# A two-layer hybrid model on one core: the second layer's modulation vector moves from TensorE to VectorE, with other first loads, slot sizes and orders

## The chip, the cores and the metric

The kernel runs on one core of a Trainium2 chip. The time is device microseconds (us) of one execution. Three runs of the kernel before are known, and one execution taken with the profiler. Engines are named as in the profile: PE is TensorE, DVE is VectorE, ACT is ScalarE, POOL is GpSimd, SP is the engine that issues the DMAs.

## What is computed

Two layers over 384 tokens (128 of a prompt, 256 latent ones), model width 1024, all in fp32. From the reference, cut:

```python
mod_ctx = silu(c_ctx) @ w_ada[l] + b_ada[l]     # for the 128 prompt tokens
mod_lat = silu(c) @ w_ada[l] + b_ada[l]         # for the 256 latent tokens
shift1, scale1, gate1, shift2, scale2, gate2 = split(mod, 6)
h = rms_norm(x) * (1 + scale1) + shift1
out = mix(h)     # w_in; SSD scan, attention and mLSTM side by side; gated merge; w_out
x = x + gate1 * out
h = rms_norm(x) * (1 + scale2) + shift2
a_, b_ = split(h @ w_ffn_in, 2)                 # 2 x 2816 columns
x = x + gate2 * ((silu(a_) * b_) @ w_ffn_out)
# after both layers: final rms_norm; also new k, v and the scans' end states
```

The piece that matters most here is the first pair of lines ("adaLN"): per layer two vectors of 1024 (prompt and latent) times a matrix of 1024 x 6144. It depends on c and c_ctx alone, not on x.

## The kernel before, in words

All large weights come in one stream `ws` of pieces of 128 x 1024 floats (512 KB), in the order in which `stream()` (line 64) lists them. A piece is loaded into one of four buffers `raw`. To keep fp32 precision, it is split into a high part (`wh`, a rounding copy on ACT) and a low part (`wl` = raw - wh, a subtraction on DVE, or on POOL for the pieces that `POOL_SPLIT` names, one of so many of a kind). The activations are split in the same way: `HH` and `HL`, in the FFN the slots `A` and `C`. A dense product of one piece is 24 matmuls: eight blocks of 128 rows, each high by high, high by low and low by high, over 384 columns (386 with the slots A and C, which carry two more) into one of `ND` = 3 PSUM tiles `d`.

The stages of a layer are: input projections and the three branches interleaved with gates, the branches' projections (`br`), the output projection (`out`), then the FFN: `ff` with 44 pieces, `fa` and `fb` in turn, and `fo` with 22. In ff, each tile d is evacuated on DVE (`sc<-d,nacc`), a product of the two halves is made (`sc<-sc,sc`), the shift of the modulation is added (a pair of `sc<-sc,sh,sc`, 128 and 256 columns), and the hidden block is split into high and low part (`F<-sc,F` and the like for other slots).

adaLN. Layer 0's first pieces are wanted at once: `ada` (line 733) runs 16 pieces through PE at the start, 4 x 4, with the conditioning `silc` (32 columns, two used) as one operand, and transposes what comes out. The rest is done in steps, `ada_step` (line 754): 2 pieces, 8 matmuls `m<-raw,silc`; after 8 steps ScalarE copies the rows out, and four transposes with an addition of the bias `bada` bring the result into columns `mod`. There are 40 steps. 16 are layer 0's and lie in the branches' projections, 24 are layer 1's and lie in layer 0's FFN, 16 in ff and 8 in fo.

What sets the order. All operations are first recorded (`Recorder.rec`, which is why nearly every row of the profile names line 509, where they are emitted) and then ordered by `order()` (line 376): a list scheduler with a table of costs, in which a ready operation with the lowest key goes first. The key is the place in the program plus an urgency: `FEED` (weights), `EVAC` (evacuations), `DENSE`. The result is a fixed list per engine, and each engine runs its own list in order; an instruction that waits holds up all behind it. All DMAs go through SP's list. SBUF slots have letters (`A` to `F2`, `K`, `HH`, `HL`, `PH`, `PL`) and are used for different things in turn; at the start only `PH` (the input x) is in use of the large ones.

At the seam from `out` to the FFN, `outproj` (line 1358) adds the gated result to x and sums squares; `norm_end` (835) forms the reciprocal root (a chain of small DVE operations on 128 x 3, `rs`), spreads it over partitions with a matmul (`m<-sc,ones`), and ACT stores it as `nacc`. FFN matmuls start before that, on unnormalised data; the evacuation multiplies by `nacc`.

Of the kernel before, what the change touches and what calls it, by code (L numbers as in the profile page):

```python
# [31 lines left out]
EARLY_GATES = (0, 1, 2, 4, 5, 5, 6, 6, 6, 10, 11, 13, 13, 23, 32, 32, 32, 33, 33, 37, 37, 37, 37, 38)  # L32
# [31 lines left out]
def stream():  # L64
# [3 lines left out]
    for l in range(LAYERS):  # L68
# [18 lines left out]
        s += spread(ff, steps(l + 1, 0, 1)) + spread(fo, steps(l + 1, 2)) if l + 1 < LAYERS else ff + fo  # L87
# [135 lines left out]
class Recorder:  # L223
# [152 lines left out]
    def order(self):  # L376
# [25 lines left out]
        port = ring = 0.0  # L402
# [133 lines left out]
MIX = "sssiiiqqqsqqmamsasqamsasammmaamam"  # L536

POOL_SPLIT = {"inn": 4, "fa": 3, "fo": 3}


class Net:
    def __init__(self, ctx, tc, I, O):
# [237 lines left out]

    def setup(self):
# [8 lines left out]
        self.badas = []  # L790
        for l in range(LAYERS):
            b = self.const(f"bada{l}", [P, 48])
            self.dma(b, I["cols"][l, :, COLS["bada"][0]:COLS["bada"][0] + 48])
            self.badas.append(b)
# [813 lines left out]
```

## Time and profile before

| | us |
|---|---|
| median of 3 runs | 1937.8 (1936.15 to 1947.53) |
| the profiled execution | 1940.55, its span 1938.4, mean granted clock 0.994 |
| PE busy in the span | 1894.3 (98%) |
| DVE busy | 1290.6 (67%) |
| ACT busy | 945.6 (49%) |
| POOL busy | 367.1 (19%) |

PE's 98% is the first thing to read: nearly all of the time is matmul time, with short holes. Matmuls are pipelined, so a row's length (0.34 us) is longer than the distance to the next start (0.17 us); distances between starts give the pace. The same holds for DVE, where a row ends a little after the next one starts. A timeline row shows start, length, engine, line, operation, and in brackets how long the engine was idle before it and what ended that.

### The profile page before, as it was taken

The numbers are of one execution on the slowest core, as the hardware profiler recorded it, in microseconds if no ns is written. First come the engines' busy times: TensorE is split into PE (matmuls) and PEld (weight loads), VectorE is DVE, ScalarE is ACT, GpSimd is POOL, SyncE is SP. The second block draws the span as 40 slices with busy tenths as digits, with TensorE's granted clock in tenths as the row PEclk, the third lists the DMA queues.
The fourth block names the chain that finished last, engine by engine and source line by source line (L and its number), as shares of the span: only waits on it lengthen the run. The fifth ranks groups of instructions, "written<-read, shape, count | busy, mean of one in ns | idle before, by whom it ended". The sixth has DMA issues, their size and how long they took to land. (4 is left out here: it accounts for less than half of the span.)

```text
span 1938.4 us, 30576 instructions
## 1 busy us (share of the span) xinstructions
PE 1894.3 (98%) x11202; PEld 1728.1 (89%) x11202; DVE 1290.6 (67%) x2733; ACT 945.6 (49%) x1910; POOL 367.1 (19%) x355
## 2 busy tenths in 40 slices
PE   6999999999999999999999999999999999999997
PEld 4998898688888999999999978986889999999997
DVE  3856887986745666565348668978867567666622
ACT  3655565765422444444336546656655434444421
POOL 0115432210102210000211234322100022000121
PEclk9999999999999999999999999999999999999998
DMA  8466555554578666666654655555544555444441
GB/s 302 122 178 190 148 150 147 141 147 129 172 262 267 223 196 185 196 201 201 192 178 144 156 170 150 158 147 135 144 124 140 161 169 160 120 125 124 131 125 61
DMA packets 120342, 318.33 MB, mean 164 GB/s; under 512 B 13824, under 2 KB 57216, under 8 KB 119424
## 3 DMA queue, kind: packets, MB, share of 16 engines
q1 hardware_dynamic: 120192, 316.38, 54.8%
q8 instruction: 88, 1.44, 0.3%
q14 instruction: 62, 0.51, 0.1%
HBM read 295.54 MB, written 19.74 MB: 163 GB/s over the span
## 5 line engine op out<-in xcount | busy, mean ns | idle before, releaser
L509 ACT ACTIVATE wh<-raw 128x1024 fp32r<-128x1024 f32 x374 | 396.0, 1059 | 566.8 <-PE d L509 509.1
L509 DVE TENSOR_TENSOR wl<-raw,wh 128x1024 fp32r<-128x1024 f32 x335 | 437.3, 1306 | 247.3 <-ACT wh L509 240.4
L509 PE MATMUL d<-HH,wh 128*128 128x384 f32 x1448 | 493.0, 348 | 2.6 <-ACT sc L509 1.6
L509 PE MATMUL d<-HL,wh 128*128 128x384 f32 x1416 | 467.9, 336 | 1.4 <-DVE HL L509 1.4
L509 PE MATMUL d<-HH,wl 128*128 128x384 f32 x1384 | 465.6, 336 | 0.7 <-DVE wl L509 0.7
L509 PEld LDWEIGHTS d<-HH,wh 128*128 128x128 f32 x1448 | 272.6, 189 | 22.8 <-issue 14.8
L509 PEld LDWEIGHTS d<-HL,wh 128*128 128x128 f32 x1416 | 266.8, 189 | 3.2 <-DVE HL L509 1.7
L509 PEld LDWEIGHTS d<-HH,wl 128*128 128x128 f32 x1384 | 261.0, 189 | 1.1 <-DVE wl L509 1.1
L509 PE MATMUL d<-A,wh 128*128 128x386 f32 x744 | 254.8, 342 | 0.0
L509 PE MATMUL d<-C,wh 128*128 128x386 f32 x744 | 251.5, 338 | 0.0
L509 PE MATMUL d<-A,wl 128*128 128x386 f32 x744 | 250.1, 336 | 0.0
L509 POOL TENSOR_TENSOR wl<-raw,wh 128x1024 fp32r<-128x1024 f32 x39 | 93.9, 2409 | 449.6 <-ACT sh L509 361.3
L509 PEld LDWEIGHTS d<-A,wh 128*128 128x128 f32 x744 | 139.9, 188 | 13.0 <-issue 10.9
L509 PEld LDWEIGHTS d<-C,wh 128*128 128x128 f32 x744 | 140.6, 189 | 0.4
L509 PEld LDWEIGHTS d<-A,wl 128*128 128x128 f32 x744 | 139.9, 188 | 0.0
L509 POOL TENSOR_TENSOR sc<-sc,sc 128x126 f32<-128x126 f32 x112 | 66.7, 614 | 253.9 <-DVE sc L509 195.9
L509 DVE TENSOR_TENSOR sc<-d,nacc 128x384 f32<-128x384 f32 x93 | 51.8, 557 | 78.9 <-PE d L509 74.6
L509 DVE SCALAR_TENSOR_TENSOR PH<-PL,n,cst 128x128 f32<-128x128 f32 x288 | 95.9, 366 | 7.7 <-PE m L509 5.2
L509 PE MATMUL d<-wh,HH 128*128 128x512 f32 x240 | 98.2, 409 | 0.0
L509 PE MATMUL d<-wl,HH 128*128 128x512 f32 x240 | 93.9, 391 | 0.0
L509 PE MATMUL d<-wh,HL 128*128 128x512 f32 x240 | 93.8, 391 | 0.0
L509 DVE SCALAR_TENSOR_TENSOR sc<-d,cw,sc 128x127 f32<-128x127 f32 x224 | 79.2, 408 | 14.9 <-ACT sc L509 14.4
(237 smaller groups left out, 3080.1 us busy)
## 6 DMA issues: line engine op xcount, KB each, us to landing
raw<-in_ws SPq DMA_DIRECT2D x470, 512.0 KB, 3.9
PL<-rowr SPq DMA_DIRECT2D x48, 384.0 KB, 5.7
gd<-sc SPq DMA_DIRECT2D x48, 192.0 KB, 2.0
pb<-gd SPq DMA_DIRECT2D x48, 192.0 KB, 2.9
ex<-rowe SPq DMA_DIRECT2D x32, 128.0 KB, 4.1
ex<-rowe SPq DMA_DIRECT2D x16, 256.0 KB, 5.5
PH<-in_xT SPq DMA_DIRECT2D x2, 1536.0 KB, 7.2
yad<-pb SPq DMA_DIRECT2D x16, 192.0 KB, 3.0
```

Of the source, the lines that this page charges most:

```text
L509: tc.keep_in_program_order(getattr(engines[op.eng], meth)(*[real(a) for a in args], **{k: real(v) for k, v in kw.items()}))
```

## The change

1. *Layer 1's adaLN* is no longer done in steps on PE. Its 48 pieces come as 48 blocks (`ada_block`): each gives 128 columns of the result for both vectors by two scalar_tensor_tensor on DVE, raw times a row that is the same in all partitions (silu of c or c_ctx, read back from DRAM into the slot `PL`), with the sum over the row written to `mod`. 32 blocks lie in ff and 16 in fo. The weights are laid out anew for it.
2. *First loads.* The 16 first pieces no longer go through `raw` but come in six DMAs of two or three pieces into the slots A, C, E, F, D, PL, the first eight pieces with urgency `FIRST` and the last eight with `SECOND`; three pieces of the dense work load between them. The two bias loads come later; the setup has urgency `FIRST`.
3. *Norms* (`ssq` at the start, `norm_end`) get the urgency `NORM`, ahead of FEED.
4. *FFN low parts* of the hidden blocks of layer 0 (22 of 128 x 384) go from DVE to POOL, and `POOL_SPLIT` keeps only fo, now every second piece.
5. *Slots*: A, C and E get 3136 floats per partition, a multiple of 256 bytes, and the large slots a pool of their own with a pad of 64 bytes ahead.
6. *Order*: another interleaving of the branches (`MIX`), one gate one place earlier, and other costs in the scheduler.

```diff
-EARLY_GATES = (0, 1, 2, 4, 5, 5, 6, 6, 6, 10, 11, 13, 13, 23, 32, 32, 32, 33, 33, 37, 37, 37, 37, 38)
+EARLY_GATES = (0, 1, 2, 4, 5, 5, 6, 6, 6, 10, 11, 13, 13, 23, 31, 32, 32, 32, 33, 33, 37, 37, 37, 38)
...
-        s += spread(ff, steps(l + 1, 0, 1)) + spread(fo, steps(l + 1, 2)) if l + 1 < LAYERS else ff + fo
+        if l + 1 < LAYERS:
+            blocks = [(("adv", l + 1, place, j), 1) for place in range(6) for j in range(8)]
+            at = len(blocks) * len(ff) // len(ff + fo)
+            s += spread(ff, blocks[:at]) + spread(fo, blocks[at:])
+        else:
+            s += ff + fo
...
+            if "accum_out" in kw:
+                n += 60
...
-            return 0.36, rows * (0.025 + run * 4 * 0.0000415) / 16, 1.3 + min(rows, 256) * 0.0085
+            return 0.36, rows * (0.036 + run * 4 * 0.0000337) / 16, 1.3 + min(rows, 256) * 0.0085
...
+NORM = -90000
+
+FIRST, SECOND = -120000, -110000
...
+BIG = ("A", "B", "C", "D", "E", "F", "F2", "K", "HH", "HL", "PH", "PL")
+PADS = dict(p1=0, p2=64)
...
+AHEAD_OF_SECOND = 3
+
+FIRST_LOADS = ((0, 3, "A"), (3, 3, "C"), (6, 2, "E"), (8, 3, "F"), (11, 3, "D"), (14, 2, "PL"))
...
-MIX = "sssiiiqqqsqqmamsasqamsasammmaamam"
-
-POOL_SPLIT = {"inn": 4, "fa": 3, "fo": 3}
+MIX = "ssiiiqqqaqqmamsasqmssasasmmmaamam"
+
+POOL_SPLIT = {"fo": 2}
...
     def ada(self, l, u):
-        raws = self.piece(("ada", l, u), split=False)
+        key, cnt = self.stream[self.spos]
+        assert key == ("ada", l, u), key
+        self.spos += 1
+
+        if self.ppos % 8 == 0:
+            with self.urgency(SECOND if self.ppos else FIRST):
+                for pos, n, tag in FIRST_LOADS:
+                    if pos // 8 == self.ppos // 8:
+                        home = self.slot(tag, [P, n, 1024])
+                        self.dma(home.rearrange("p n c -> p (n c)"),
+                                 self.I["ws"][pos:pos + n].rearrange("n p c -> (n p c)").rearrange("(p m) -> p m", p=P))
+                        self.homes += [home[:, i] for i in range(n)]
+        raws = [self.homes.pop(0) for _ in range(cnt)]
...
+    def ada_block(self, kind, l, place, j):
+
+        if self.spos == self.adv_at:
+            t = self.slot("PL", [P, 3, D])
+            self.dma(t[:, 0:2], self.sild.rearrange("r p k -> r (p k)").unsqueeze(0).to_broadcast([P, 2, D]))
+            self.silb = t
+        raw, = self.piece((kind, l, place, j), split=False)
+        with self.urgency(FEED):
+            for r in range(2):
+                self.nc.vector.scalar_tensor_tensor(self.silb[:, 2] if r == 0 else raw, raw, 1.0, self.silb[:, r],
+                                                    ALU.mult, ALU.mult, accum_out=self.mod_col(l, place, j, r))
...
-            self.xs = [self.slot(t, [P, KT, NTOK + 2], F32R) for t in "AC"]
+            self.xs = [self.slot(t, [P, 3136], F32R)[:, 0:3088].rearrange("p (k n) -> p k n", k=KT) for t in "AC"]
...
-                self.tt(homes[j][:, 1], th, homes[j][:, 0].bitcast(F32), ALU.subtract)
+                (self.ptt if l == 0 else self.tt)(homes[j][:, 1], th, homes[j][:, 0].bitcast(F32), ALU.subtract)
...
-            self.norm_end(EPS)
+            with self.urgency(NORM):
+                self.norm_end(EPS)
```

How the lists move is seen at three places. In the rows the first number behind a name is the buffer, the second the version.

*The start, on PE.* Before, the last matmuls of `ada` read two `raw` buffers that are loaded one after the other, and dense matmuls (HH by wh) follow a transposition:

```order
L509 MATMUL d_37_315<-raw_33_266,silc_7_82 32x128 x8
L509 MATMUL d_37_315<-raw_34_276,silc_7_82 32x128 x8
L509 MATMUL m_58_346<-sc_57_334,ones_6_78 128x384
L509 MATMUL d_37_315<-raw_35_287,silc_7_82 32x128 x8
L509 MATMUL d_37_315<-raw_36_302,silc_7_82 32x128 x8
L509 MATMUL d_39_386<-cst_3_95,sc_38_382 128x128
L509 MATMUL d_73_407<-HH_60_368,wh_71_389 128x384
L509 MATMUL d_73_407<-HL_61_380,wh_71_389 128x384
L509 MATMUL d_73_407<-HH_60_368,wl_72_399 128x384
L509 MATMUL d_73_407<-HH_60_368,wh_71_389 128x384
```

In the change (line 516 now) the last sixteen read what one DMA brings into the slot PL, and three dense matmuls stand ahead of the transposition:

```order
L516 MATMUL d_27_308<-F_24_115,silc_8_93 32x128 x24
L516 MATMUL d_27_308<-D_25_117,silc_8_93 32x128 x8
L516 MATMUL d_30_361<-D_25_117,silc_8_93 32x128 x4
L516 MATMUL d_29_366<-cst_3_95,sc_28_359 128x128
L516 MATMUL d_30_361<-D_25_117,silc_8_93 32x128 x12
L516 MATMUL d_30_361<-PL_26_119,silc_8_93 32x128 x16
L516 MATMUL d_66_399<-HH_53_299,wh_64_254 128x384
L516 MATMUL d_66_399<-HL_54_304,wh_64_254 128x384
L516 MATMUL d_66_399<-HH_53_299,wl_65_269 128x384
L516 MATMUL d_32_403<-cst_3_95,sc_31_397 128x128
```

What moved: the operands are slots that are filled by six loads, and the dense product begins behind the last of them as before.

*The entry of layer 0's FFN, on DVE.* Here `rs` and `r` are the end of the reciprocal root, `sc<-cst,r` makes the matrix that PE spreads, `sc<-d,nacc` is an evacuation. Before:

```order
L509 SCALAR_TENSOR_TENSOR r3_1322_7359<-rs_1325_7338,rs_1326_7332 128x3
L509 TENSOR_SCALAR sc_1327_7361<-cst_3_95,r3_1322_7359 128x128 x2
L509 TENSOR_TENSOR wl_1362_7369<-raw_1360_7237,wh_1361_7351 128x1024
L509 TENSOR_SCALAR sc_1327_7361<-cst_3_95,r3_1322_7359 128x128
L509 TENSOR_TENSOR sc_1344_7395<-d_1342_7291,nacc_1321_7390 128x384
L509 TENSOR_TENSOR sc_1350_7411<-d_1348_7347,nacc_1321_7390 128x384
L509 SCALAR_TENSOR_TENSOR sc_1351_7418<-sc_1351_7418,sc_1344_7395 128x384
L509 SCALAR_TENSOR_TENSOR sc_1351_7418<-sc_1350_7411,sh_1349_7416,sc_1351_7418 128x128
```

In the change:

```order
L516 SCALAR_TENSOR_TENSOR r3_1315_7391<-rs_1318_7361,rs_1319_7346 128x3
L516 TENSOR_SCALAR sc_1320_7396<-cst_3_95,r3_1315_7391 128x128 x3
L516 TENSOR_TENSOR wl_1354_7405<-raw_1352_7221,wh_1353_7388 128x1024
L516 TENSOR_TENSOR wl_1362_7416<-raw_1360_7254,wh_1361_7400 128x1024
L516 SCALAR_TENSOR_TENSOR PL_1329_6954,mod1_13_7102<-raw_1374_7372,PL_1329_6954 128x1024
L516 TENSOR_TENSOR wl_1369_7432<-raw_1367_7335,wh_1368_7425 128x1024
L516 SCALAR_TENSOR_TENSOR raw_1374_7372,mod1_13_7102<-raw_1374_7372,PL_1329_6954 128x1024
L516 TENSOR_TENSOR sc_1336_7437<-d_1334_7268,nacc_1314_7420 128x384
L516 TENSOR_TENSOR sc_1343_7441<-d_1341_7299,nacc_1314_7420 128x384
L516 TENSOR_TENSOR sc_1351_7449<-d_1349_7357,nacc_1314_7420 128x384
L516 SCALAR_TENSOR_TENSOR sc_1344_7451<-sc_1344_7451,sc_1336_7437 128x384
L516 SCALAR_TENSOR_TENSOR sc_1344_7451<-sc_1343_7441,sh_1342_7411,sc_1344_7451 128x128
```

What moved: between the reciprocal root and the first evacuation stood one wl, now there are three and two sums over `PL` and `raw` (one block); the evacuations of three tiles follow one another, and the next block comes behind them.

*The same place on PE.* Before, a step of layer 1's adaLN (`m<-raw,silc`) stands just ahead of the spreading matmul `m<-sc,ones`:

```order
L509 MATMUL d_1348_7347<-A_1283_7020,wh_1346_7251 128x386
L509 MATMUL d_1348_7347<-C_1284_7025,wh_1346_7251 128x386
L509 MATMUL d_1348_7347<-A_1283_7020,wl_1347_7262 128x386
L509 MATMUL m_1338_7139<-raw_1373_7274,silc_7_82 32x512 x2
L509 MATMUL m_1338_7139<-raw_1374_7317,silc_7_82 32x512 x2
L509 MATMUL m_1328_7381<-sc_1327_7361,ones_6_78 128x384
L509 MATMUL d_1348_7347<-A_1283_7020,wh_1346_7251 128x386
L509 MATMUL d_1348_7347<-C_1284_7025,wh_1346_7251 128x386
L509 MATMUL d_1348_7347<-A_1283_7020,wl_1347_7262 128x386
```

In the change:

```order
L516 MATMUL d_1349_7357<-A_1276_7011,wh_1347_7274 128x386
L516 MATMUL d_1349_7357<-C_1277_7019,wh_1347_7274 128x386
L516 MATMUL d_1349_7357<-A_1276_7011,wl_1348_7286 128x386
L516 MATMUL m_1321_7407<-sc_1320_7396,ones_7_91 128x384
L516 MATMUL d_1349_7357<-A_1276_7011,wh_1347_7274 128x386
L516 MATMUL d_1349_7357<-C_1277_7019,wh_1347_7274 128x386
L516 MATMUL d_1349_7357<-A_1276_7011,wl_1348_7286 128x386
L516 MATMUL d_1349_7357<-A_1276_7011,wh_1347_7274 128x386
L516 MATMUL d_1349_7357<-C_1277_7019,wh_1347_7274 128x386
L516 MATMUL d_1349_7357<-A_1276_7011,wl_1348_7286 128x386
L516 MATMUL d_1355_7444<-A_1276_7011,wh_1353_7388 128x386
```

What moved: the step is gone, as are all others of layer 1; behind the spreading matmul six matmuls complete the third tile, and then a fourth tile `d` begins, in the buffer of one of the three.

## Rows read from the trace of the kernel before

**Rows 1.** The page's first line and its part 1.
```profile
span 1938.4 us, 30576 instructions
...
PE 1894.3 (98%) x11202; PEld 1728.1 (89%) x11202; DVE 1290.6 (67%) x2733; ACT 945.6 (49%) x1910; POOL 367.1 (19%) x355
```

**Rows 2.** Busy time by stretch (columns: stretch, length, busy per engine, PEclk, DMA share, GB/s).
```profile
20.00:40.00 20.00, 16.87 (x187) 10.56 (x180) 8.37 (x34) 5.78 (x13) 1.97 (x6) 0.98 0.89 302
...
712.00:905.00 193.00, 193.00 (x1121) 176.19 (x1120) 118.41 (x166) 85.57 (x170) 15.45 (x7) 1.00 0.62 194
905.00:1000.00 95.00, 95.00 (x558) 88.23 (x557) 36.84 (x49) 32.18 (x47) 23.12 (x13) 1.00 0.59 184
```

**Rows 3.** The tile raw on PE: duration min/median/max, first and last start.
```profile
L509 PE MATMUL m<-raw,silc x320: 592/605/617, 524.4 to 977.9; 128*32 128x512 f32 x160
```

**Rows 4.** PE timeline around one adaLN step (start, length, engine, operation).
```profile
690.77 0.34 PE L509 MATMUL d<-HH,wl 128*128 128x384 f32 x1
691.04 1.10 PE L509 MATMUL m<-raw,silc 128*32 128x512 f32 x8
692.07 0.44 PE L509 MATMUL d<-HH,wh 128*128 128x384 f32 x1
692.35 0.34 PE L509 MATMUL d<-HL,wh 128*128 128x384 f32 x1
```

**Rows 5.** PE timeline at the entry of layer 0's FFN; DVE's first evacuation.
```profile
698.59 0.34 PE L509 MATMUL d<-A,wh 128*128 128x386 f32 x1
...
700.70 0.72 PE L509 MATMUL m<-ones,sc 128*128 128x1 f32 x6
...
706.69 0.91 PE L509 MATMUL m<-sc,ones 128*128 128x384 f32 x2
...
708.22 0.56 DVE L509 TENSOR_TENSOR sc<-d,nacc 128x384 f32<-128x384 f32 x1 [2.10 <-ACT nacc L509]
```

**Rows 6.** Groups on DVE in 712 to 905, shapes apart (busy, mean ns).
```profile
L509 DVE TENSOR_TENSOR wl<-raw,wh 128x1024 fp32r<-128x1024 f32 x35 | 42.9, 1226 | 12.6 <-ACT wh L509 12.5
L509 DVE TENSOR_TENSOR sc<-d,nacc 128x384 f32<-128x384 f32 x41 | 22.9, 557 | 43.4 <-PE d L509 43.4
```

**Rows 7.** DVE timeline, two instructions back to back.
```profile
68.77 1.22 DVE L509 TENSOR_TENSOR wl<-raw,wh 128x1024 fp32r<-128x1024 f32 x1
69.91 0.55 DVE L509 SCALAR_TENSOR_TENSOR A<-sc,sc 128x384 f32<-128x384 f32 x1
```

**Rows 8.** ACT timeline, a summing instruction's readout and the next instruction.
```profile
314.39 0.19 ACT L509 ACTIVATION_READ_ACCUMULATOR s<-xn 128x1 f32 x1
314.49 0.30 ACT L509 ACTIVATE s<-xn 128x128 f32<-128x128 f32 x1
```

**Rows 9.** DVE timeline, an undisturbed and a disturbed pair; POOL beside the latter.
```profile
713.56 0.75 DVE L509 SCALAR_TENSOR_TENSOR sc<-sc,sh,sc 128x128 f32<-128x128 f32 x2
...
822.01 2.91 DVE L509 SCALAR_TENSOR_TENSOR sc<-sc,sh,sc 128x128 f32<-128x128 f32 x2 [0.42 <-ACT sh L509]
...
821.99 2.39 POOL L509 TENSOR_TENSOR wl<-raw,wh 128x1024 fp32r<-128x1024 f32 x1 [25.29 <-ACT sh L509]
```

**Rows 10.** Groups on POOL, shapes apart.
```profile
L509 POOL TENSOR_TENSOR nacc<-nacc,sc 128x384 f32<-128x384 f32 x24 | 27.5, 1145 | 112.5 <-ACT sc L509 112.5
```

**Rows 11.** PE timeline from the last start matmuls to continuous dense work.
```profile
34.40 1.78 PE L509 MATMUL d<-raw,silc 128*32 128x128 f32 x32
...
38.00 0.44 PE L509 MATMUL d<-HH,wh 128*128 128x384 f32 x1 [1.03 <-ACT wh L509]
...
44.46 0.44 PE L509 MATMUL d<-HL,wh 128*128 128x384 f32 x1 [1.40 <-DVE HL L509]
```

**Rows 12.** DMA of the first 60 us in 40 equal slices.
```profile
GB/s 0 153 363 412 405 364 412 442 311 312 403 410 418 237 282 238 276 322 369 385 330 281 347 276 295 276 300 254 232 303 156 191 0 0 11 0 0 139 341 396
```

**Rows 13.** PE timeline, a wait in layer 1's branches.
```profile
1142.60 0.69 PE L509 MATMUL m<-pb,bn 128*64 128x128 f32 x4 [3.35 <-POOL pb L509]
```

**Rows 14.** Groups on DVE over the whole span, shapes apart.
```profile
L509 DVE SCALAR_TENSOR_TENSOR D<-sc,sc 128x384 f32<-128x384 f32 x16 | 9.1, 566 | 2.9 <-ACT sc L509 2.9
```

More of the change, by code (lines that the diff above doesn't have):

```diff
@@ L401, in order @@
         pe = self.Clock()
-        port = ring = 0.0
+        port, ring = 0.0, 2.2
         def offer(i, t):
@@ L642, in piece @@
             ahead = self.stream[self.spos][0]
-            (self.early_gate if ahead[0] == "gate" else self.ada_step)(*ahead)
+            dict(gate=self.early_gate, ada=self.ada_step, adv=self.ada_block)[ahead[0]](*ahead)
         want, cnt = self.stream[self.spos]
@@ L649, in piece @@
                 raw = self.buf("wp", "raw", [P, 1024], NR)
-                self.dma(raw, self.I["ws"][self.ppos])
+                with self.urgency(FIRST if self.ppos < 16 + AHEAD_OF_SECOND else FEED):
+                    self.dma(raw, self.I["ws"][self.ppos])
                 self.ppos += 1
@@ L746, in ada @@
         self.nc.tensor.transpose(ps2[:, 0:P], st, self.ident)
+        if u == 0:
+            with self.urgency(FIRST):
+                for i, b in enumerate(self.badas):
+                    self.dma(b, self.I["cols"][i, :, COLS["bada"][0]:COLS["bada"][0] + 48])
         src = ps2[:, 0:P].rearrange("p (j r) -> p j r", j=4)[:, :, 0:2]
@@ L779, in ada_step @@
                 self.ts(v, v, 0.5, ALU.mult)
+    def ada_block(self, kind, l, place, j):
[8 more added lines that the diff above has]
+                                                    ALU.mult, ALU.mult, accum_out=self.mod_col(l, place, j, r))
+        if j < 7:
+            return
+        v = self.mod[l % 2][:, 8 * place:8 * place + 8]
+        self.tt(v, v, self.badas[l][:, 8 * place:8 * place + 8].unsqueeze(2).to_broadcast([P, 8, 2]), ALU.add)
+        if place in (SCALE1, SCALE2):
+            self.ts(v, v, 1.0, ALU.add)
+        elif place in (GATE1, GATE2):
+            self.ts(v, v, 0.5, ALU.mult)
     def setup(self):
@@ L789, in setup @@
         self.ident = self.cst("ident")
[L790 to L794, printed above, removed]
+        self.homes = []
+        self.badas = [self.const(f"bada{l}", [P, 48]) for l in range(LAYERS)]
         self.dma(self.x, I["xT"])
+        for n, size in PADS.items():
+            if size:
+                nc.gpsimd.memset(self.buf(n, n, [P, size // 4], 1), 0.0)
         self.ones = self.const("ones", [P, P])
@@ L803, in setup @@
         self.stt(self.silc[:, :, 0:2], th, 1.0, ct, ALU.add, ALU.mult)
+        rows = self.slot("sil2", [P, 2, KT])
+        self.act(rows, self.silc[:, :, 0:2].rearrange("p k r -> p r k"), AF.Copy)
+        self.sild = self.dram("sild", [2, P, KT])
+        with self.urgency(0):
+            self.dma(self.sild.rearrange("r p k -> p r k"), rows)
+        self.adv_at = [k[0] for k, _ in self.stream].index("adv")
         self.mod = [self.const(f"mod{i}", [P, 48, 2]) for i in range(2)]
@@ L1412, in run @@
     def run(self):
-        self.setup()
+        with self.urgency(FIRST):
+            self.setup()
         for u in (0, 2, 1, 3):
             self.ada(0, u)
-        for j in range(8):
-            self.ssq(self.x[:, j], j, self.tt)
+        with self.urgency(NORM):
+            for j in range(8):
+                self.ssq(self.x[:, j], j, self.tt)
         self.xd = self.I["xT"]
@@ L1427, in run @@
             self.ts(self.mlnh, self.col("mln", 0, 8), 0.5, ALU.mult)
-            self.norm_end(EPS)
+            with self.urgency(NORM):
+                self.norm_end(EPS)
             self.gd = self.dram("gd", [P, 24, NTOK])
@@ L1449, in run @@
             self.outproj(l, m)
-            self.norm_end(EPS)
+            with self.urgency(NORM):
+                self.norm_end(EPS)
             self.ffn(l)
@@ L1530, in layout @@
             v = w_ada[l, key[3]].reshape(P, 6, D)[:, [CHUNKS[2 * key[2]], CHUNKS[2 * key[2] + 1]]]
+        elif kind == "adv":
+            c = CHUNKS[key[2]] * D + key[3] * P
+            v = w_ada[l][:, :, c:c + P].transpose(2, 1, 0)
         elif kind == "br":
@@ L1542, in layout @@
         pos += n
+    for at, n, _ in FIRST_LOADS:
+        ws[at:at + n] = ws[at:at + n].transpose(1, 0, 2).reshape(n, P, 1024)
     out["ws"] = ws
```

7 lines of the change are left out of this document (4 added, 3 removed).

## The prediction, made before the change was run

> **What bounds the kernel now.** I read the page's busy line first [rows 1]: TensorE (PE) is busy 1,894 of 1,938.4 us, VectorE (DVE) 1,291, ScalarE 946, GpSimd (POOL) 367. So the kernel is a chain of matmuls, and a change can win in three ways: fewer matmuls, fewer holes, or an earlier first dense matmul. It can lose where another engine stops feeding PE. The busy time by stretch [rows 2] shows where that is near: in 712 to 905, most of layer 0's ff stage, PE is busy without a hole and DVE for 118 of 193 us; in 905 to 1000 (fo) for 37 of 95. Before the first dense matmul PE is busy 16.9 us in 20 to 40 while the DMA engines are 89% busy. The profiled execution took 1940.55 us, 2.75 (0.14%) above the median of 1937.8; I sum against it and subtract 2.75 at the end.
>
> **1. Layer 1's adaLN leaves PE: -30.5 us.** The tile view has 320 matmuls of the kind m<-raw,silc [rows 3], 8 per step, so 40 steps; 24 of them are layer 1's and go, layer 0's 16 stay. One step's price is read at 690.77 [rows 4]: from the dense matmul before it to the second one behind it pass 1.58 us. Two dense intervals are 0.35 (twelve of them fill 698.59 to 700.70, 0.176 each [rows 5]), so a step costs 1.23 us, and 24 cost 29.5. The 12 transposes that go with them are 128 columns each: an estimate of 1 us from the 384-column interval.
>
> **2. The same work arrives on DVE.** 96 scalar_tensor_tensor of 128x1024 with a sum: 63 are issued between the first and last evacuation of layer 0's ff, the other 33 around and behind it. What one costs (call it a) no row shows. The nearest is wl<-raw,wh, also 1,024 columns with two SBUF operands: 1.23 us long [rows 6], and the next starts 1.14 after it [rows 7]. That is the lower end. A sum has to be read out; on ScalarE the trace shows that as an extra instruction, 0.19 us long, 0.10 until the next starts [rows 8]. So I take a = 1.14 + 0.10 = 1.24, 1.34 as the likely upper end, and 2.28, twice the wl interval, as the far one.
>
> DVE's work from the first to the last ff evacuation, each at its row less the 0.09 by which neighbours overlap [rows 7]: 44 evacuations at 0.47 [rows 6] = 20.5; 40 wl at 1.14 = 45.6 (the change takes ff's low parts off POOL); 22 products at the same 0.47 = 10.3; 22 pairs sc<-sc,sh,sc at 0.66 (0.75 undisturbed, 713.56 [rows 9]) = 14.5; small ones 0.7; 63 sums at 1.24 = 78.1. Together 169.7.
>
> The 22 hidden low parts that go to POOL block DVE as well. At 821.99 [rows 9] POOL's wl took 2.39, and the DVE pair that started beside it took 2.91 for 0.75: DVE lost 2.16 of POOL's 2.39, a share of 0.9. Not each DVE instruction has two SBUF operands, so I take 0.7, ends 0.5 and 0.9, of about 1 us each (384 columns on POOL are 1.15 [rows 10]): 15.4. DVE needs 185.1 us. PE, with three PSUM tiles already full when evacuation begins, has 41 pieces of 24 matmuls left, 41 x 24 x 0.1758 = 173.0. **DVE sets the pace of this stage, and 12.1 us come back** (1.4 at a = 1.14 and 0.5; 22.8 at a = 1.34 and 0.9). What is late next is PE, waiting for a free PSUM tile behind an evacuation that is queued behind sums.
>
> **3. The seam into that stage: +4.** Before, DVE has only one wl between the rsqrt chain and the first evacuation, which starts 1.5 us after m<-sc,ones [rows 5]. Now three wl and two sums stand there: 3 x 1.14 + 2 x 1.24 = 5.9 us. PE meanwhile has only six matmuls (1.1 us) before it needs the tile of that evacuation. 5.9 + 0.5 for it, less 1.1 and some dispatch, is 4 to 5; ends 2 and 6. The two sums inside the chain cost nothing: PE has 42 matmuls (7.4 us) between m<-ones,sc and m<-sc,ones, and the chain with them is 2.6 + 2.5 + the C and sc operations, about 7.
>
> **4. fo: +3.** DVE 36.8 us in 95 before [rows 2], 39 over the whole stage of 92 + 8 steps x 1.23 = 102; four wl fewer (POOL now takes every second), -4.6; 33 sums, +40.9: 75. POOL is busy 23 now, 34 with four more wl; at the shares 0.3 to 0.9 that is 10 to 31 of blocked DVE. So 85 to 106 against 22 x 24 x 0.174 = 92 of PE: 0 to 8 with what spills into layer 1's modulation, 3 taken.
>
> **5. The start: -5.5.** Now the last ada matmuls begin at 34.40, the first dense one at 38.00, and dense work is continuous from 44.46 with 13 dense matmuls done [rows 11]; as if it had begun at 44.46 - 13 x 0.174 = 42.2. In the change PE's order puts all ada matmuls ahead of the first dense one, the last 16 on the slot PL. Ahead of and in PL's load stand x, A, C, F, D (1,536 KB each), E and PL (1,024 KB), three pieces, constants: 11.8 MB. The rate: 302 GB/s at 0.89 busy [rows 2] is 339 at full share, and single slices reach 403 to 418 [rows 12]. At 380, with 2.4 us until bytes flow, PL is there at 33.4 and dense work begins at 34.4, 7.8 earlier. A stretch of half-rate matmuls like the one between 38.00 and 44.46 may stay, 13 x 0.15 = 1.9. Taken 5.5; ends 2 (at 339) and 10 (at 410).
>
> **6. Nothing, with what hides it.** Without POOL's inn and fa parts, 17 wl more come to DVE and 22 lows leave: +19.4 - 10.3, and with 119 of sums DVE is at 1,419 us, 74%; outside layer 0's FFN it has the cover of PE's work. The new MIX and gate place move waits like that at 1142.60 (3.35 us for POOL's pb [rows 13]) either way: 0, ends -5 and 5. Slot sizes: the intervals with A and C (0.176) and with HH (0.174) differ by 0.002, half of which the two extra columns explain; over 93 pieces of 24 that is at most 2.2 us. Norm urgency and later bias loads lie in terms 3 and 5.
>
> **Sum:** -30.5 + 12.1 + 4 + 3 - 5.5 = -16.9; 1940.55 - 16.9 = 1923.7, less 2.75: **1921 us**, 0.9% faster. A measurement of this kernel tells about 1%, 19 us, from no change.
>
> **The rivals.**
> - *DVE keeps up.* a = 1.14, share 0.5, POOL's work mostly beside evacuations: ff gives back 1.4, the seam 2, fo nothing; -27 and -7.8 at the start, about **1903**. For it: DVE idles 75 us of 193 now. Against: 63 sums use these up. Chance 0.20.
> - *The low parts and POOL's fo pieces block DVE fully.* Share 0.9 at a = 1.24: ff gives back 16.5, the seam 6, fo 8: nothing of the 30.5 is left, and the start alone remains: **1932**. For it: the 2.91 [rows 9]. Chance 0.13.
> - *The start does not move* because the DMA engines are full now already (0.89), and large rows carry no more bytes: term 5 is 0, the rest as forecast: **1926**. Against it: slices of 282 and less stand beside slices of 410 [rows 12]. Chance 0.07.
> - *The sum costs a second pass: slower.* If a scalar_tensor_tensor with two SBUF operands and a sum runs at half rate, a = 2.28. ff: 91.6 + 143.6 + 15.4 = 251 against 173, +78; fo: 34 + 75 + 20 = 129 against 92, +37; seam +6. With -30.5 and -5.5 that is +85: about **2023**. The point from which this decides: all terms add to zero at a = 1.41, and the kernel is slower by over 1% from 1.61. Against it: without a sum the same instruction with two SBUF operands takes 566 ns at 384 columns [rows 14], no more than the plain two-operand evacuation with its 557 [rows 6]. For it: the sum is just what no row has. Chance 0.10. The Trainium skill, "Vector Engine (DVE) Microarchitecture Reference", section "7. Points that are easy to get wrong", says that this instruction with two non-bf16 SBUF sources halves throughput, with no read port left for the accumulator's readback. Taken for every such instruction the trace speaks against it (566 ns against 557); with a sum no run here shows it, and by it the time would be this rival's.
>
> **How the numbers follow.** The forecast has 0.50; its own range is 1910 to 1932, with the 1% line (1918.4) inside: 0.25 faster, 0.25 within. Rival one is all faster (0.20); rival two within 0.11 and slower 0.02, since sums above 1.6 would come on top of it; rival three within 0.07; rival four slower. Faster 0.45, within 0.43, slower 0.12. The low end is rival one with 2 us of the reorder on top, 1901; the high end all upper terms at once, -30.5 + 22.8 + 6 + 8 - 2 = +4.3, 1942; the last rival and the tails stay out.
>
> **What would show it.** Right: m<-raw,silc falls to 128 matmuls and PE's busy time by about 30; the sums stand near 1.25 us; in layer 0's ff PE shows holes ended by DVE's evacuations, together 10 to 20 us, and DVE is busy over 95%; the stage opens with a hole of some 4 us; the first HH matmul comes before 36 us. Wrong: sums of 2 us or more; a ff stage without holes; the first HH matmul at 38 or later; holes over 5 us where there were none, in the branches.

## The result and the profile after

The changed kernel takes 1913.2 us (median of 4 runs, 1910.7 to 1916.8) against 1940.1 for the kernel before in the same comparison: ratio 0.986, 95% interval 0.982 to 0.990. That is 27 us less, where the prediction had 17. The profiled execution took 1915.68 us, 24.9 less than that of before. First the page's first line and its part 1, to be held against [rows 1], then the stretches that answer to [rows 2] (ff of layer 0, then fo):

```profile
span 1913.9 us, 30335 instructions
...
PE 1866.6 (98%) x10998; PEld 1727.5 (90%) x10998; DVE 1375.4 (72%) x2923; ACT 945.1 (49%) x1905; POOL 361.4 (19%) x361
```

```profile
712.20:889.60 177.40, 176.68 (x984) 176.71 (x985) 162.85 (x267) 81.34 (x163) 31.05 (x21) 0.98 0.65 206
889.00:982.00 93.00, 93.00 (x541) 93.00 (x540) 73.21 (x105) 34.37 (x50) 39.60 (x18) 1.00 0.66 205
```

PE is busy 28 us less, DVE 85 us more, and the span shrinks by 24.5: nearly all that left PE was gained. The steps of layer 1 are gone: of the 320 matmuls of [rows 3], the 128 of layer 0 are left.

```profile
L516 PE MATMUL m<-raw,silc x128: 592/605/617, 522.0 to 639.7; 128*32 128x512 f32 x128
```

In ff DVE is busy 163 of 177 us (92%), and still PE has no hole but one. Where the time went is read best from the stages. The table's lengths are distances between starts on PE: the 61st dense matmul, the first and last FFN matmul with A in a layer, the last matmul of all.

| stretch (us) | before | changed | early evacuations (e4) | steps on PE (e5) |
|---|---|---|---|---|
| to the 61st dense matmul | 52.7 | 46.6 | 45.6 | 46.8 |
| on to layer 0's first FFN matmul | 645.9 | 647.3 | 644.5 | 649.6 |
| ff of layer 0 | 206.9 | 195.7 | 189.8 | 208.5 |
| on to layer 1's first gate (fo) | 100.4 | 92.4 | 92.4 | 100.2 |
| on to layer 1's ff | 638.6 | 636.5 | 633.2 | 631.8 |
| ff of layer 1 | 186.7 | 188.3 | 188.3 | 188.3 |
| to the last matmul | 99.3 | 99.2 | 99.2 | 99.2 |

A second profile of the unaltered change (e1) has 646.6, 633.7 and 194.7 in the second, fifth and third line. Over e1, e2, e4, e8, e9 and e11, which have the change's order in the branches, the second line goes from 642.4 to 649.7 and the fifth from 633.2 to 636.2: the branches differ by up to 7 and 3 us from one profile to the next, and nothing is read from less there.

**The sums.** The view of the tile raw on DVE shows what [rows 6, 7, 8] could only bound (duration ns min/median/max, first and last start):

```profile
L516 DVE TENSOR_TENSOR wl<-raw,wh x352: 1153/1225/2102, 20.9 to 1883.0; 128x1024 fp32r<-128x1024 f32 x176
L516 DVE SCALAR_TENSOR_TENSOR PL<-raw,PL x48: 1211/1220/3291, 676.5 to 962.9; 128x1024 f32<-128x1024 f32 x48
L516 DVE DVE_READ_ACCUMULATOR PL<-raw,PL x48: 74/82/89, 677.9 to 964.0; 128x1 f32 x48
```

A sum over two SBUF operands lasts 1,220 ns in the median, a plain subtraction wl 1,225. The readout is there as an instruction of its own, as on ScalarE, but the DVE timeline at the seam shows what it costs the engine:

```profile
706.52 2.36 DVE L516 TENSOR_TENSOR wl<-raw,wh 128x1024 fp32r<-128x1024 f32 x2 [0.40 <-ACT wh L516]
708.80 1.22 DVE L516 SCALAR_TENSOR_TENSOR PL<-raw,PL 128x1024 f32<-128x1024 f32 x1
709.94 0.08 DVE L516 DVE_READ_ACCUMULATOR PL<-raw,PL 128x1 f32 x1
709.94 1.22 DVE L516 TENSOR_TENSOR wl<-raw,wh 128x1024 fp32r<-128x1024 f32 x1
711.08 1.22 DVE L516 SCALAR_TENSOR_TENSOR raw<-raw,PL 128x1024 f32<-128x1024 f32 x1
712.22 0.09 DVE L516 DVE_READ_ACCUMULATOR raw<-raw,PL 128x1 f32 x1
712.22 1.49 DVE L516 TENSOR_TENSOR sc<-d,nacc 128x384 f32<-128x384 f32 x3
```

At 709.94 the readout and the next wl start together: from one sum to the next instruction it is 1.14 us, the readout costs nothing. So a = 1.143, the lower end, where the forecast had 1.24. The same rows are the seam: two wl, a sum, a wl, a sum stand ahead of the first evacuation at 712.22. On PE:

```profile
708.47 0.33 PE L516 MATMUL d<-A,wl 128*128 128x386 f32 x1
712.92 0.66 PE L516 MATMUL d<-A,wh 128*128 128x386 f32 x1 [4.12 <-DVE sc L516]
713.38 0.53 PE L516 MATMUL d<-C,wh 128*128 128x386 f32 x1
...
717.88 0.48 PE L516 MATMUL d<-A,wh 128*128 128x386 f32 x1
718.20 0.34 PE L516 MATMUL d<-C,wh 128*128 128x386 f32 x1
```

The hole ends with the evacuation, 4.45 us after the last start instead of 0.18, the one wait of that size in layer 0's FFN. And it has an echo: behind it starts are 0.32 us apart until 717.88, some 15 matmuls that lose 0.14 us each. The windows of that stretch and of the one behind it (the number ahead of the DMA share is the granted clock) show why, half the clock, 1.2 of 2.4 GHz, and then all of it:

```profile
713.40:717.80 4.40, 4.40 (x15) 4.40 (x14) 3.72 (x7) 2.53 (x6) 1.51 (x1) 0.50 0.52 199
718.40:722.40 4.00, 4.00 (x24) 4.00 (x23) 3.14 (x7) 1.12 (x2) 0.00 (x0) 1.00 0.38 131
```

The length of the echo is not fixed: in e1 the same hole, again 4.45 us, ends at 712.21, and the clock is 0.50 to 715.3 only, 3.1 us in place of 5.3. That is about the 1 us by which ff differs in the two profiles.

**Who waits at the shared SBUF access.** The first low part in POOL's timeline, and the two sums that ran beside it in DVE's:

```profile
716.23 1.51 POOL L516 TENSOR_TENSOR D<-sc,D 128x384 fp32r<-128x384 f32 x1 [18.81 <-ACT D L516]
```

```profile
715.65 1.22 DVE L516 SCALAR_TENSOR_TENSOR PL<-raw,PL 128x1024 f32<-128x1024 f32 x1
...
716.92 1.90 DVE L516 SCALAR_TENSOR_TENSOR raw<-raw,PL 128x1024 f32<-128x1024 f32 x1
```

Here POOL takes 1.51 us for what takes 1.01 in e5, where DVE has no sums, and DVE 1.90 for 1.22. POOL came while the sum from 715.65 ran, the next sum came while POOL ran, and each was late by about the rest of the other. Between the first and the last evacuation of ff the profile has 20 low parts on POOL. 15 of them took longer than 1.02 us, 8 us more than undisturbed in all, and five DVE instructions beside them did, by 4 us; with one sum beside a wl of POOL it is 4.4 us for DVE, about 0.2 us per low part. (e9 below, worked out from DVE's busy time, gives 6 us, 0.3 each.) In [rows 9] DVE had lost 2.16 of POOL's 2.39 us: there POOL had started 0.02 us ahead of it. In the full queue it is mostly POOL that waits. The Trainium skill, "SBUF — State Buffer", section "Who interferes with whom", says that issue order decides who blocks; these rows agree.

DVE's waits in ff of layer 0 (us in total, times, longest) show that it had room: in 16 places it had caught up with PE and waited for a product.

```profile
DVE sc L516 <- PE d L516: 7.7, 16, 1.5
DVE wl L516 <- ACT wh L516: 3.2, 11, 0.4
```

**The start.** Rows of PE that answer to [rows 11], and the DMA row that answers to [rows 12]:

```profile
27.68 2.79 PE L516 MATMUL d<-F,silc 128*32 128x128 f32 x48 [4.53 <-DMA F<-in_ws]
...
34.51 1.54 PE L516 MATMUL d<-PL,silc 128*32 128x128 f32 x32
35.98 0.45 PE L516 MATMUL d<-HH,wh 128*128 128x384 f32 x1
...
46.61 0.34 PE L516 MATMUL d<-HH,wh 128*128 128x384 f32 x1
```

```profile
GB/s 0 136 365 369 426 451 426 410 434 407 431 361 407 431 464 396 401 426 434 396 396 360 148 104 171 306 404 285 16 0 11 131 224 385 131 300 14 131 169 180
```

From 5 to 30 us the DMA engines move mostly 400 to 464 GB/s, where before it was 237 to 442: 417 on average against 352, and their busy share is full in both (1.01 and 0.98). The first dense matmul comes 2.0 us earlier, the 61st 6.1 (52.72 before), because nothing waits behind it: no half-rate stretch, no wait for HL. The half-rate stretch of the start (granted clock 0.50) lies from 25.3 to 35.5 us now, over the waits for F and D and the last `ada` matmuls; before it lay from 39.3 to 42.7, over dense ones.

### The profile page after: what moved, and what is told of

Read it like the earlier page. It is cut to its first block, busy times and chain, and to the rows that moved or that the text cites. A ratio compares the mean times of both kernels' runs of the same rounds, so it can differ in the third digit from the quotient of the medians.

```text
span 1913.9 us, 30335 instructions
## 1 busy us (share of the span) xinstructions
PE 1866.6 (98%) x10998; PEld 1727.5 (90%) x10998; DVE 1375.4 (72%) x2923; ACT 945.1 (49%) x1905; POOL 361.4 (19%) x361
## 5 line engine op out<-in xcount | busy, mean ns | idle before, releaser
L516 DVE TENSOR_TENSOR wl<-raw,wh 128x1024 fp32r<-128x1024 f32 x352 | 454.9, 1293 | 226.8 <-ACT wh L516 224.1
L516 POOL TENSOR_TENSOR sc<-sc,sc 128x126 f32<-128x126 f32 x112 | 61.7, 570 | 272.4 <-DVE sc L516 159.9
L516 DVE SCALAR_TENSOR_TENSOR PH<-PL,n,cst 128x128 f32<-128x128 f32 x288 | 102.6, 389 | 14.5 <-PE l L516 5.3
L516 POOL TENSOR_TENSOR wl<-raw,wh 128x1024 fp32r<-128x1024 f32 x22 | 55.4, 2516 | 270.7 <-ACT sh L516 193.1
L516 PE MATMUL d<-PH,wh 128*128 128x384 f32 x256 | 87.1, 340 | 0.0
L516 PE MATMUL d<-PH,wl 128*128 128x384 f32 x256 | 86.0, 336 | 0.0
```

The lines of the kernel that those rows point to most:

```text
L516: tc.keep_in_program_order(getattr(engines[op.eng], meth)(*[real(a) for a in args], **{k: real(v) for k, v in kw.items()}))
```

## The experiments

All medians are of 4 runs (5 for e5); each ratio is to the kernel before, run beside it. e1 to e4 share one comparison, e5 to e8 another, e9 to e12 a third.

**e1, the change again.** 

> The changed kernel once more, unaltered, as the yardstick beside the other three. Both theories: 1911 to 1917 us, the first HH matmul at 36 us, one hole of 4.5 us at the entry of layer 0's FFN, intervals of 0.177 us between FFN matmuls in both layers.

 Measured: 1912.7 us, ratio 0.985 (0.983 to 0.987), hole and intervals as before.

**e2, the old slot sizes.** The edit, cut (the last line is the slot E of a branch):

```diff
-PADS = dict(p1=0, p2=64)
+PADS = dict(p1=0, p2=0)
...
-        return self.buf("bp" if tag in BIG else "sp", tag, shape, 1, dt)
+        return self.buf("sp", tag, shape, 1, dt)
...
-            self.xs = [self.slot(t, [P, 3136], F32R)[:, 0:3088].rearrange("p (k n) -> p k n", k=KT) for t in "AC"]
+            self.xs = [self.slot(t, [P, KT, NTOK + 2], F32R) for t in "AC"]
...
-        self.mv = self.slot("E", [P, 3136])[:, 0:3096].rearrange("p (t h d) -> p t h d", t=3, h=8)
+        self.mv = self.slot("E", [P, 3, 8, 129])
```

> Only the slot sizes and pads of before; the order of every engine is that of the changed kernel. Theory A (the sizes themselves slow the FFN matmuls: the intervals in layer 1's ff, whose work is the same in both kernels, went from 0.1755 to 0.1771 us): intervals fall back to 0.1755 in both ff stages, 93 pieces of 24 gain 3.6 us. Theory B (the slower intervals come from what DVE, POOL and the DMAs do beside them, or from that one execution): intervals stay at 0.177, time unchanged within 1 us.

 Measured: 1911.0 us, 0.984 (0.982 to 0.987), ff of layer 1 188.6 us. No difference, and the intervals stayed. But this did not separate the theories: in this kernel A still starts at 224 above a multiple of 256 bytes, as in the change. e8 and e11 settle it.

**e3, part 1 alone.** The kernel before with the blocks in the stream, `ada_block`, the rows of silu through DRAM and the weights' layout for them:

```diff
-        s += spread(ff, steps(l + 1, 0, 1)) + spread(fo, steps(l + 1, 2)) if l + 1 < LAYERS else ff + fo
+        if l + 1 < LAYERS:
+            blocks = [(("adv", l + 1, place, j), 1) for place in range(6) for j in range(8)]
...
```
 

> The kernel before with part 1 of the change alone: layer 1's adaLN on DVE, all else as before (FFN low parts on DVE, seven of ff's wl on POOL). Its list has one sum, not three wl and two sums, ahead of the first evacuation. Theory A (the gain is the 24 steps' PE time, and a sum costs DVE no more than a wl, 1.14 us): the sums cost 1.14 again and the entry hole is under 1 us. DVE's work in ff is 20.6 + 42.3 + 24.8 + 10.3 + 63 x 1.14 = 170, and if POOL's seven wl block it at the share 0.9 another 15: 185 against 174 of PE, so 11 come back and 3 in fo, 31 - 14 = 17 us faster than before, about 1922; if POOL's work hides, 27 faster, about 1912. Theory C (most of the gain is in the first loads and the order): at most 10 us faster, 1928 or more.

 Measured: 1921.7 us, 0.9895 (0.987 to 0.992). The total is the expected one, the way to it is not. ff without its holes took 192 us (half-rate matmuls behind them included), so the sums and POOL's wl cost little there; what costs is the entry, where holes of 6.1 and 2.4 us stood instead of under one. The timelines of DVE, POOL and PE there:

```profile
708.73 2.36 DVE L516 TENSOR_TENSOR rs<-rs,rs 128x3 f32<-128x3 f32 x1
```

```profile
708.58 2.48 POOL L516 TENSOR_TENSOR wl<-raw,wh 128x1024 fp32r<-128x1024 f32 x1 [8.52 <-ACT sh L516]
```

```profile
716.60 1.65 PE L516 MATMUL m<-sc,ones 128*128 128x384 f32 x2 [5.77 <-DVE sc L516]
719.81 0.66 PE L516 MATMUL d<-A,wh 128*128 128x386 f32 x1 [1.56 <-DVE sc L516]
```

An instruction of 128 x 3 elements with two SBUF operands, started 0.15 us behind POOL's wl, took 2.36 us and ended with it, and sums and wl stand within the reciprocal root. Part 1 without parts 3 and 4 has a dearer seam.

**e4, the seam.**

```diff
-                with self.urgency(EVAC):
+                with self.urgency(NORM if l == 0 and j < 2 else EVAC):
                     sh = self.ring("sh", [P, 2], 4)
```

> The changed kernel with one urgency altered: the evacuations of the first two blocks of layer 0's ff go ahead of wl and sums, so that two wl, and no sum, stand between the norm and the first evacuation. Theory A (the hole of 4.45 us at 708 is the evacuation queued behind three wl and two sums): the hole shrinks to about 1 us and the kernel is 3.4 us faster than the unaltered one. Theory B (DVE is at its limit through ff, so what is put off there is only paid later): the hole shrinks but holes of the same sum open further on, no gain.

 Measured: 1904.3 us (1903.1 to 1907.7), 0.981 (0.979 to 0.983), 8.5 less than e1. The timelines of DVE and PE at the entry:

```profile
702.80 2.36 DVE L516 TENSOR_TENSOR wl<-raw,wh 128x1024 fp32r<-128x1024 f32 x2 [0.44 <-ACT wh L516]
705.08 1.01 DVE L516 TENSOR_TENSOR sc<-d,nacc 128x384 f32<-128x384 f32 x2
```

```profile
705.68 0.45 PE L516 MATMUL d<-A,wh 128*128 128x386 f32 x1 [0.60 <-DVE sc L516]
```

The hole is 0.93 us from start to start, the half-rate stretch is gone, and no other hole opened: ff is 4.9 us shorter than in e1. Theory A holds. The rest of the 8.5, 3.6 us, has no cause that is shown: in the profiles of e4 and e1 it lies in the start (1.0) and the branches (2.5), where every engine's order is the same in both. This version beats both kernels.

**e5, the steps back on PE.** The same line of the stream the other way round, without `ada_block`:

```diff
-            s += spread(ff, blocks[:at]) + spread(fo, blocks[at:])
+        s += spread(ff, steps(l + 1, 0, 1)) + spread(fo, steps(l + 1, 2)) if l + 1 < LAYERS else ff + fo
```

> The changed kernel without part 1: layer 1's adaLN in 24 steps on PE again, all other parts kept. Theory A (part 1 is worth the PE time of the 24 steps, 30.5 us, less the 4.5 us hole and about 2 in fo): 24 us slower than the changed kernel, some 1937 us. Theory C (most of the 27 us come from first loads and order): at most 10 us slower, under 1924. The forecast's terms (12 us come back in ff) would give 11 to 12 slower, 1925.

 Measured: 1933.5 us, 0.996 (0.995 to 0.998). Part 1 is worth 20.4 us, between the theories' 24 and 11.5 and nearer the first. Against e4, which has no entry hole, ff is 18.7 and fo 7.8 us longer: 24 steps cost 26.5, 1.17 each in ff and 0.98 in fo, transposes with them.

**e6, the old first loads.** `ada` takes its pieces from `raw` again, the bias loads come early again, and the urgencies go (cut):

```diff
-                with self.urgency(FIRST if self.ppos < 16 + AHEAD_OF_SECOND else FEED):
+                with self.urgency(FEED):
...
-        raws = [self.homes.pop(0) for _ in range(cnt)]
+        raws = self.piece(("ada", l, u), split=False)
...
-        with self.urgency(FIRST):
-            self.setup()
+        self.setup()
```

> The changed kernel without part 2: first pieces through raw, bias loads and setup as before. Theory A: the 60th dense matmul starts at 52.7 us again instead of 46.6, 6 us slower than the changed kernel, about 1919. Rival: the stretch behind it has waits of its own that swallow the head start, 0 to 2 us.

 Measured: 1921.3 us, 0.991 (0.989 to 0.992): 8 us slower; the 61st dense matmul starts at 57.6, even later than before. The head start is not swallowed. Taken out one at a time, parts 1 and 2 cost 20.4 and 8.1 us, about the whole gain of 27. But the 8.1 is not what part 2 brought: with the old loads the rest of the change starts its dense work 4.9 us later than the kernel before does, and why is not shown. Against the kernel before, the start gained the 6.1 us of the table.

**e7, more sums.**

```diff
+                if r == 0:
+                    self.nc.vector.scalar_tensor_tensor(self.silb[:, 2], raw, 1.0, self.silb[:, r],
+                                                        ALU.mult, ALU.mult, accum_out=self.mod_col(l, place, j, r))
```

> The changed kernel with one sum of each block done twice (48 more on DVE, 32 of them in ff, at 1.14 us each: 36.6 us in ff, 18.3 in fo); its list has no sum ahead of the first evacuation, so the entry hole of 4.5 us should be gone. Theory A (in ff DVE needs 163.6 us at 1.143 a sum and 6 for POOL, against 174 to 177 of PE, so it has 4 to 8 us of room): ff gets 29 to 32 us longer less the 4.5 of the hole, fo 0 to 8; 25 to 35 slower, about 1940. If POOL blocked DVE at the forecast's share 0.7 (15 us), there would be no room and ff would be 35 to 40 longer. Rival D (DVE has much room and its work hides): under 15 slower.

 Measured: 1951.5 us, 1.006 (1.0045 to 1.0075), 38 slower than the change, a little over the upper end; ff 231.7 (+36.0), fo 99.2 (+6.8). The window over ff, and the largest of its waits on PE:

```profile
694.00:925.00 231.00, 203.82 (x1067) 200.72 (x1066) 217.23 (x372) 88.42 (x177) 29.42 (x21) 0.90 0.56 172
```

```profile
838.54 0.66 PE L516 MATMUL d<-A,wh 128*128 128x386 f32 x1 [6.63 <-DVE sc L516]
```

The largest group of PE's waits there (us in total, times, longest):

```profile
PE d L516 <- DVE sc L516: 16.0, 4, 6.6
```

DVE is full (217 of 231 us) and PE waits for evacuations; the granted clock falls to 0.90. The hole at the entry did not vanish: there the modulation of A and C waited behind the sums, 4.1 and 1.6 us. So the room in the change is small: 36.6 us more of sums made ff 36.0 us longer. PE waits 27 us in this ff, all groups together, where in the change it waits 4.4; the rest fits the half-rate stretches.

**e8 and e11, where A and C start.** e8 is e4 without the pad, e11 has in addition

```diff
-            self.xs = [self.slot(t, [P, 3136], F32R)[:, 0:3088].rearrange("p (k n) -> p k n", k=KT) for t in "AC"]
+            self.xs = [self.slot(t, [P, dict(A=3112, C=3136)[t]], F32R)[:, 0:3088].rearrange("p (k n) -> p k n", k=KT) for t in "AC"]
```

> The kernel with the early evacuations (1904 us) with the pad ahead of the large slots taken out, so that A, C and all large slots start at 160 instead of 224 above a multiple of 256 bytes. A was at 160 in the kernel before, whose intervals between FFN matmuls were 0.1755 us, and at 224 in all later ones (0.1770 to 0.1775); the intervals that follow a matmul with A are the ones that grew. Theory A (where A starts decides): 0.1755 again in both ff stages and 3 to 4 us less, about 1901. Theory B (something else in these executions): 0.177 stays, no change within 1 us.

 

> The kernel with the early evacuations, A at 160 and C at 64 above a multiple of 256 bytes as in the kernel before (slot A is given 3112 floats, the pad is taken out). With A and C both at 160 a trio of FFN matmuls took 0.5291 us, with both at 224 0.5316, in the kernel before 0.5267. Theory A (only where the two slots start decides): 0.5267 in both ff stages, 2 to 4 us less than with 224, 1901 us. Theory B (the kernel before had something else): 0.529 stays.

 Measured: 1904.0 (0.981, 0.979 to 0.982) and 1903.6 us (0.982, 0.980 to 0.984): neither differs from e4's 1904.3. In the trace the matter is clear all the same. Layer 1's ff has the same work in all kernels; its first and last matmuls with A, in the change, e8 and e11 (before: 1644.4 to 1831.1):

```profile
L516 PE MATMUL d<-A,wh x352: 334/339/637, 1618.4 to 1806.4; 128*128 128x386 f32 x176
L516 PE MATMUL d<-A,wl x352: 332/338/343, 1618.8 to 1806.8; 128*128 128x386 f32 x176
```

```profile
L516 PE MATMUL d<-A,wh x352: 335/339/634, 1611.7 to 1798.9; 128*128 128x386 f32 x176
L516 PE MATMUL d<-A,wl x352: 332/338/343, 1612.1 to 1799.2; 128*128 128x386 f32 x176
```

```profile
L516 PE MATMUL d<-A,wh x352: 335/339/633, 1605.6 to 1791.9; 128*128 128x386 f32 x176
L516 PE MATMUL d<-A,wl x352: 332/336/341, 1605.9 to 1792.2; 128*128 128x386 f32 x176
```

That is 188.3, 187.5 and 186.6 us, before 186.7. The mean distances from one trio of matmuls (A by wh, C by wh, A by wl) to the next, in undisturbed stretches, are 0.5316 us with both slots at 224 above a multiple of 256 bytes, 0.5291 with both at 160, 0.5267 with A at 160 and C at 64, and 0.5267 before with these same starts. e2 had 0.5325 (224 and 32), e3 0.5308 (224 and 128). Where the two operands start decides, and the kernel before's pair of starts brings its distance back; over 744 trios the change gives away 3.6 us by it. Which rule lies behind it stays open. That part of the change costs, and it is too small for the medians.

**e9, the low parts back on DVE.** 

```diff
-                (self.ptt if l == 0 else self.tt)(homes[j][:, 1], th, homes[j][:, 0].bitcast(F32), ALU.subtract)
+                self.tt(homes[j][:, 1], th, homes[j][:, 0].bitcast(F32), ALU.subtract)
```

> The changed kernel with layer 0's FFN low parts on DVE again (22 of 128 x 384, 10.3 us), POOL_SPLIT as changed. Theory A (in ff POOL costs DVE only 6 us, since DVE runs nearly without a break and POOL waits for it): DVE gets 10.3 - 6 = 4 us more in ff, which its 14 idle us there take up for the most part: 0 to 4 us slower. The forecast's share of 0.7 (15.4 us of blocking): DVE gets 5 us less to do, and the kernel is up to 5 faster where DVE sets the pace. Rival (nothing there matters): 0.

 Measured: 1911.0 us, 0.985 (0.983 to 0.987), no difference. The window, to be held against that of the change over the same 177.4 us, above:

```profile
712.20:889.60 177.40, 177.24 (x992) 176.95 (x992) 166.91 (x285) 81.30 (x165) 3.12 (x2) 0.99 0.64 208
```

DVE's busy time grows by 4.1 us (162.85 to 166.91), as theory A had it, POOL's falls to 3, and PE does not notice. (In e9 ff ends 2 us earlier; from the first to the last evacuation the busy times are 164.4 in the change and 168.4.) 22 low parts at 0.47 are 10.3 us, so POOL had cost DVE some 6. Part 4's low parts are worth nothing here.

**e10, the old order of the branches.** 

```diff
-MIX = "ssiiiqqqaqqmamsasqmssasasmmmaamam"
+MIX = "sssiiiqqqsqqmamsasqamsasammmaamam"
```

and `EARLY_GATES` as before: against the change three gates lie one, one and four places later, not one gate by one place. 

> The changed kernel with the old interleaving of the branches and the old place of one gate. Parts 1 and 2, taken out one at a time, cost 20.4 and 8.4 us, 28.8 together, where the change as a whole brings 27. Theory A (the order of the branches is worth nothing, and the starting places of A and C cost 2 to 4): 0 within 3 us of the changed kernel, 1910 to 1916; the waits of 3.4 us for POOL's pb in layer 1 and of 1 to 2 elsewhere come back in other places. Theory C (the new order takes those waits out): 4 to 8 us slower, 1917 to 1921.

 Measured: 1915.6 us (1911.7 to 1919.7), 0.988 (0.986 to 0.990). Some 2.5 us slower, not resolved. Waits of 3.4 and 3.3 us between starts stand in its branches at 167 and 1114; the change has none above 2 us there, so the new order does remove waits like that of [rows 13]. Yet the stages are as long as in the change (645.7 and 635.2 us in the table's second and fifth line): theory A, with a doubt of 3 us.

No run takes out the norms' urgency (part 3), `POOL_SPLIT` or the scheduler's costs alone; e3 lacks every part but the first.

**e12, one dense piece ahead of the second loads.** To e11 is added

```diff
-AHEAD_OF_SECOND = 3
+AHEAD_OF_SECOND = 1
```

> The same as the kernel with A at 160 and C at 64, and AHEAD_OF_SECOND 1 instead of 3: only one piece of dense work is loaded between the first six loads' halves, two come behind PL. Theory A (the first dense matmul waits for the bytes ahead of PL): 1 MB less at some 415 GB/s, PL and the first dense matmul 2.5 us earlier, at 33 to 33.5 us; the two pieces behind it land 2.5 us later and their split takes 2.3, which PE covers with the first piece: 1 to 2.5 us faster. Rival (the split of the late pieces becomes the wait): first dense matmul earlier, a hole of 1 to 3 us behind it, no gain.

 Measured: 1903.1 us, 0.981 (0.979 to 0.982), as e11. PE:

```profile
32.14 0.44 PE L516 MATMUL d<-HH,wh 128*128 128x384 f32 x1
...
51.95 0.55 PE L516 MATMUL m<-cst,A 128*128 128x128 f32 x3 [1.52 <-DVE A L516]
```

The first dense matmul comes at 32.1, earlier than expected, so the bytes ahead of PL do set it. The 61st comes at 43.5 (e11 45.3), and then a wait for DVE at 51.95 takes that back. The rival's outcome, though not at its place.

## Why the prediction was right, and where not

The direction, the source of the gain (PE loses the steps' time) and the range held; the size was 10 us short, and one mechanism, the one in bold, did not hold: DVE does not set the pace of ff. Of its own signs, the 128 matmuls, PE's 28 us, the 4 us hole at the entry and a first HH matmul before 36 us (35.98) came; holes of 10 to 20 us in ff and a DVE busy over 95% (92%) did not. By its steps:

- *Term 1, the steps on PE, -30.5.* 26.5 measured (e5 against e4). The price of 1.23 was read in the output projection [rows 4]; in fo a step costs 0.98.
- *Term 2, DVE sets the pace in ff, +12.1.* This is the step that failed: it measured under 1 us (ff in e4 is 189.8 us, 0.75 of that the hole at the entry; layer 1's ff, without any sums, takes 188.3 in the same kernel). Three of its numbers were too high. 1.24 for a sum was 1.143. POOL's share of 0.7 was 0.2 to 0.3, 9 to 11 us less. And 58 sums, not 63, lie between the first and the last evacuation (12 ahead, 26 behind), 12 us less with the lower price. 185.1 becomes 162 to 164, and DVE is busy 164.4 us there, under PE's 173. The stage did come close to the limit: e7 shows what 36.6 us more do.
- *Term 3, the seam, +4.* 4.3 in the hole; with the half-rate stretch behind it, which the prediction had not counted, 4.9 (e1) to 5.9 against e4, where 0.8 of a hole is left. Right in mechanism and place.
- *Term 4, fo, +3.* 0: fo is 92.4 to 92.8 us in every kernel with the sums but e7, and DVE is busy 73 us of it where 85 to 106 were expected.
- *Term 5, the start, -5.5.* -6.1 at the 61st dense matmul. In part this is luck: dense work began 1.6 us later than the 34.4 that was worked out, and the half-rate stretch of 1.9 that was allowed for behind it did not come. That the DMA engines were "89% busy" did not mean that they could move no more.
- *Term 6, nothing.* The order is worth 0 to 3. Slot starts were bounded at 2.2 us and cost 3.6: the bound compared A with HH in one kernel, where the effect depends on where A and C start, which no row of before could show.

The errors partly cancel: the gain of term 1 was 4 us too large and slot starts cost 3.6, against the 14 us or so that terms 2 and 4 gave back for nothing.

Of the rivals, the first (DVE keeps up) describes ff and fo as they are; with the seam fixed it is nearly its time, 1904 against 1903. That this is so close is luck in part, since it left out the 3.6 us of the slot starts and had 7.8 for the start, and e4 holds 3.6 us without a shown cause. The second falls with e9 and with fo's 92.4 us, the third with the 417 GB/s and e6. The fourth falls with the row of 1,220 ns against 1,225 for the plain subtraction. The Trainium skill, "Vector Engine (DVE) Microarchitecture Reference", section "7. Points that are easy to get wrong", says that two non-bf16 SBUF sources halve this instruction's throughput; read as half the rate of a plain two-operand instruction, that does not hold here for fp32 in SBUF, with a sum or without (566 ns against 557 [rows 14, 6]).

## What to carry to other kernels

When work is moved to an engine that is two thirds busy, sum its queue over the one stage that receives it, count what the stage really holds (58 sums here, not 63), and price contention by who is already running: beside 20 low parts POOL waited 15 times and the full DVE five times. Then look at the stage's entry, where the first evacuation can stand behind a whole batch of more urgent feeding; one urgency there was worth 5 us in its stage and 8.5 in the medians, where the whole change brought 27. And a hole on PE can cost more than its length: behind the one of 4.3 us the matmuls ran at half rate, behind the one of 0.8 us in e4 they did not.

## What the runs showed of the hardware that was not expected

- A DVE sum's readout (82 ns long) does not delay the next instruction: 1.143 us from sum to next in the median, 1.142 for the plain subtraction.
- The distance between fp32 matmuls over 386 columns depends on where in SBUF the moving operands start: a trio took 0.5267 to 0.5325 us for five pairs of starts, while matmuls over 384 columns with HH stayed at 0.173 to 0.174.
- The hole of 4.3 us on PE was followed by 5.3 us at half rate in one execution and by 3.1 in another (e1); the one of 0.8 us (e4) by none.
- DMA engines that were busy all of 5 to 30 us moved 352 GB/s before, with pieces of 512 KB through four buffers, and 417 in the change, with loads of 1,024 and 1,536 KB.
